# Another order of the branches and wider late products in a four-branch gated block

## The chip, the cores and the metric

One core of a Trainium2 chip. The metric is the device time of one execution in microseconds (us), the median of several runs. A profile is one execution taken by the hardware profiler; its span runs from the first to the last instruction. TensorE is written PE in the profile (PEld its weight loads), VectorE DVE, ScalarE ACT, GpSimd POOL, SyncE SP.

## What is computed

One layer over 256 tokens of width 2048. The input is RMS-normed and multiplied by a wide matrix `w_in`; the columns feed four recurrent branches of width 1024 (a: HGRN-2, b: S5, c: RWKV-7, d: Mamba-2), a z gate for each, and a sigmoid gate of width 2048 for each. Cut to what matters:

```python
h = rmsnorm(res, norm_pre[l])
(q_a, f_a, i_a, z_a, u_b, z_b, rkvwa_c, z_c, xbc_d, dt_d, z_d, gate_pre) = project_partitioned(h, w_in[l], IN_SPLITS)
o_a = hgrn2_branch(q_a, f_a, i_a, lb_all[l], hgrn_norm[l]) * silu(z_a)
o_b = s5_branch(u_b, ...) * silu(z_b)      # ends in g * sigmoid(g @ w_glu + b_glu)
o_c = rwkv7_branch(rkvwa_c, ...) * silu(z_c)
o_d = mamba2_branch(xbc_d, dt_d, z_d, ...)  # gated by silu(z_d) inside
for b in range(4):
    gate = sigmoid(gate_pre[..., b * 2048:(b + 1) * 2048] + gate_bias[l, b])
    merged += gate * (outs[b] @ w_up[l, b])
res = res + rmsnorm(merged @ w_out[l], norm_post[l])
```

All of it is float32 to near its full precision: each operand of a product is split into a high and a low part of the type float32r, and three products are summed (high x high, high x low, low x high).

## The kernel before

**The weight stream.** The weights are cut into units, each a block of output columns, and the units into 444 chunks of 512 KB. A chunk goes through four steps: SyncE issues its load into one of 3 buffers `raw` (`load`, line 1572); ScalarE copies the high part `hi` and VectorE subtracts to get `lo` (`split`, line 1584, into one of 4 buffers each); TensorE does the products into the PSUM tile `pg` of the unit (`products`, line 1595; two `pg` in turn, so a unit's PSUM must be free when the next but one begins). The loop (`loop`, line 1695) runs one step per chunk: the split of a chunk three ahead, the next load, the products, the evacuation of finished units, then branch work. A product always shows as line 261, an ACT instruction as line 207, a DVE tensor_tensor as line 216 and a scalar_tensor_tensor as line 229, since helpers issue them; the tile names tell them apart.

There are two kinds of units. A token-major unit (tm: gates, ups, z of a and d, HGRN's values, the output) has tokens as rows and 512 weight columns: a chunk is 12 matmuls of 512 columns; a unit from `w_in` or `w_out` has 8 chunks, an up unit 4. A feature-major unit (fm) has 256 features as rows and the 256 tokens as columns; the stationary operand is the weight. Its activations lie as one row of 512: 256 columns of high parts, then 256 of low ones. For each of its contraction tiles k and both f (128 features each) it does

```python
K.mm(ps[..., f, :], hi[:, kk, fs], m[:, 0:256], start=first, stop=False)
K.mm(ps[..., f, :], hi[:, kk, fs], m[:, 256:512], start=False, stop=False)
K.mm(ps[..., f, :], lo[:, kk, fs], m[:, 0:256], start=False, stop=last)
```

24 matmuls of 256 columns per chunk; 4 chunks (16 contraction tiles) per unit from `w_in`, 2 chunks (8 tiles) for the four `glu` units. The two f lie in two PSUM banks, of which they use the first half.

**The order of the units** is a list (chunks in brackets): u x4 of S5 (16), dt (2) and xbc x8 (32) of Mamba, wd (2), k x4, r x4 and v x4 of RWKV (48), q x4 and f x4 (32) and i x2 (16) of HGRN: 148 chunks. Then for d and after it for c: z (16), and four times gate and up (8 + 4 each). Then z of a (16), four gates of a (32), z of b (16), four ups of a, three gates of b, `glu` x4, the last gate of b, four ups of b, the output.

**Evacuation.** When a unit is done a generator takes it out of PSUM: `u_done` stores a copy and two parts to DRAM, `conv_done` does Mamba's convolution and stores, `shift_done` RWKV's token shift (k and r stay in SBUF, v is stored), `zfm_done` a SiLU from PSUM to `zs`, `glu_done` two sigmoids from PSUM to `ev`.

**Branches as jobs.** The recurrences are generators too, emitted between the chunks. Their matmuls go to PSUM tiles `pb`, in the same TensorE queue as the stream's. A planner books each instruction's estimated end on each engine (`t_pe`, `t_act`, `t_dve`; a transfer is booked as 2.0 us and 220 GB/s, line 181). After each chunk `run_jobs` (line 1562) emits stages of the job with the best priority, as long as

```python
while max(K.t_dve, K.t_act) <= K.t_pe + AHEAD:
```

with `AHEAD = 3.7`. Every engine works its queue in order, so what is emitted ahead of a split, or ahead of a product, stands in front of it. All loads of branches go through POOL's queue once the stream runs (`SOFT`), the weights through SP's.

Who starts when: S5's set-up (`s5_setup`, priority 5) after the constants, then S5's tiles 0 to 3 in turn, tiles 4 to 7 after job `c`; `c` (`rwkv_branch`, priority 1) when RWKV's k units are done, waiting inside for r and v; Mamba's step sizes `dt` when the dt unit is done, its halves `d0` after `dt` and `d1` after `d0` (priority 0), when the xbc units are done; HGRN's halves `a0` after `c`, `a1` after `a0` (priority 3); `b`, the reload of S5's early tiles, after `a1`. A unit may have a `need`: the first product of an up unit waits, in emission, for the branch output times its z; if the job is not done by then, `finish` (line 1550) emits all the rest of it ahead of the product.

The tiles by which a job is known in the profile: RWKV `wda`, `bc` (its keys over their norms), `L`, `GB`, `XT`, `W`, `Y`, `oc` (its output); Mamba `mx`, `mbc`, `dk` (loads), `xst`, `xD`; HGRN `hT`, `E`, `oa`; S5 `s5p` and `cx` in set-up, `us`, `bs`, `ta`, `tb`, `cu` in the tiles, `ghl` its split output.

Of the kernel before, what the change touches and what calls it, by code (L numbers as in the profile page):

```python
# [15 lines left out]
AF = mybir.ActivationFunctionType  # L16
# [47 lines left out]
AHEAD = 3.7  # L64
SLACK = 1.0

# the functions that each activation table serves
# [6 lines left out]
class _Kern:  # L74
    """Pools, constants and instruction helpers shared by the weight stream and the branches."""
# [36 lines left out]
    @staticmethod  # L112
    def live(tiles):
        """How many of the tiles are still referred to; the others are dropped from the list."""
        for i in range(len(tiles) - 1, -1, -1):
            if sys.getrefcount(tiles[i]) <= 2:
                del tiles[i]
        return len(tiles)
# [4 lines left out]
    def wait(self, n):  # L123
        """Until n more slots are free."""
        for _ in range(100):
            if self.room(n):
                return
            yield BLOCKED

    def wait_banks(self, n):  # L130
        """Until n more PSUM banks are free."""
# [5 lines left out]
    def fm(self, name, n=2):  # L137
        """A feature-major [128, 4 n, 256] array, in tiles of four feature tiles."""
        return [self.big([128, 4, 256], name=f"{name}{j}") for j in range(n)]
# [22 lines left out]
    def book(self, engine, cost, out, ins):  # L162
        """Book an instruction: it starts when the engine is free and its operands are there."""
# [45 lines left out]
    def _dve(self, out, ins, ns):  # L209
        """Book a vector instruction; one that reads the last one's output waits for it."""  # L210
# [52 lines left out]
    def tr(self, out, in_, b=0):  # L263
        """out = in_ transposed; in_ starts at partition b."""
# [12 lines left out]
    def ld(self, out, in_):  # L277
        """A transfer whose source may still be under way."""
# [3 lines left out]
    def ldx(self, out, in_):  # L282
        """A load of what has long been in DRAM."""
# [5 lines left out]
    def st(self, out, in_):  # L289
        """A store of what the scalar engine has just written."""  # L290
# [11 lines left out]
    def split(self, hi, lo, src):  # L302
        """src (float32 in SBUF) as the exact sum of two float32r parts."""
# [3 lines left out]
    def rstd(self, out, ss, n, eps):  # L307
        """out = 1 / sqrt(ss / n + eps), small tiles."""
# [5 lines left out]
def setup_consts(K):  # L314
# [24 lines left out]
    # ind[:, g, :] sums each half of the partitions into rows 2 g and 2 g + 1 of 32  # L339
# [15 lines left out]
    # lmask[s, level, t]: s and t (mod 64) are paired at that level of the binary split; level 0 is the diagonal  # L355
# [26 lines left out]
def head_sum(K, ps, i, sq):  # L382
    """Sums over each head's features of tile i, to rows 32 (i % 4) + 2 (i // 4) + half of ps."""
# [4 lines left out]
def bcast_heads(K, dst, src):  # L388
    """src DRAM [4, 4, 256] to dst (two tiles [128, 4, 256]): row (q, 2 g + e) on the 64 partitions of half e."""
# [5 lines left out]
# ---------------------------------------------------------------- RWKV-7  # L395
def rwkv_branch(K, rw):
    """rw: r, k, v (two tiles [128, 4, 256]) and wda [128, 256], after the token shift. Leaves K.o['c']."""
# [94 lines left out]
    # L1[c][e]: on the 64 key partitions of head parity e, rows (a | r) scaled by the decay;  # L492
    # on the other 64 partitions the masked products of k with them
# [37 lines left out]
    for c in range(4):  # L531
# [34 lines left out]
        # token-major copies of the scaled keys  # L566
# [89 lines left out]
    # Ws[e]: on the key partitions (state | U), on the other half (V | V)  # L656
# [31 lines left out]
    for q in range(2):  # L688
# [13 lines left out]
        for o in range(2):  # L702
# [11 lines left out]
            # the A^T blocks are no longer needed: their place takes the right-hand sides  # L714
# [88 lines left out]
# ---------------------------------------------------------------- HGRN-2  # L803
def hgrn_bounds(K):
    """The lower bounds of the forget gates, [128, 8 feature tiles]: log lb, -log lb, log(1 - lb), 1 - lb."""
    lg = K.parv("lb")
    t = K.sm([128, 5, 8], "lb")
    # softmax and running sum over the one layer, then minus the first layer's
# [19 lines left out]
def hgrn_half(K, g, load):  # L828
    """Heads 4g..4g+3: q, f [128, 4, 256] feature-major, v [128, 2, 512] token-major. Leaves K.o['a', g]."""
# [52 lines left out]
    # scores^T: the 64 x 64 diagonal blocks in accd, both off-diagonal kinds in acc and soff  # L882
# [111 lines left out]
def tail_tm(K, o, j, norm, ohl):  # L994
    """Block j (512 features) of a token-major output [128, 2, 512]: transpose, scale by norm, split."""
# [18 lines left out]
# ---------------------------------------------------------------- Mamba-2  # L1014
def mamba_steps(K, dtr):
    """Step sizes and decays of all heads from dt [16, 256]; token-major in K.mtm, running sums also in DRAM."""
# [15 lines left out]
    # dt = softplus(raw + bias) = max(x, 0) + log1p(exp(-|x|)), log1p(e) = 2 atanh(e / (2 + e))  # L1032
# [41 lines left out]
def mamba_half(K, g, load):  # L1074
    """Heads 8g..8g+7: x [128, 4, 256], bcx [128, 4, 256] (two groups' B, then C). Leaves K.o['d', g]."""
# [91 lines left out]
def mamba_tail(K, j, zs):  # L1167
    """Gate block j (512 features, two groups) and normalise; zs = silu(z) [128, 2, 512]."""
# [16 lines left out]
# ---------------------------------------------------------------- S5  # L1185
def exp_exact(K, out, x, t, ti):
    """out = exp(x) to float32 rounding: 2^k exp(r); t: two scratch tiles, ti: an int32 one."""
# [8 lines left out]
    # exp(r) = 1 + (r + r^2 / 2! + ... + r^9 / 9!)  # L1196
# [1092 lines left out]
```

## Time and profile before

| | |
|---|---|
| median of 3 runs | 1430.18 us (1429.64 to 1430.91) |
| profiled execution, span | 1427.8 us, 24645 instructions |
| profiled execution, what lies around the span | not listed; the median is 2.4 us above the span |
| PE / PEld / DVE / ACT / POOL busy | 97 / 86 / 73 / 58 / 11% of the span |
| bytes moved | 288.62 MB, mean 202 GB/s |
| matmuls of the stream with 512 columns | 393 ns mean for one (line 261, `pg<-hi,h`) |
| with 256 columns | 286 ns mean for one (`pg<-h,hi`) |

Matmuls are pipelined: the time of one overlaps the next, so the spacing of their starts is what a matmul takes from TensorE's time, not its duration. A wait is put down to the instruction that released it, in the form "engine tile line <- engine tile line: us in total, times, longest". In a table by stages a row is a stretch in us from the span's start, its length, the busy time and count of each engine, the granted TensorE clock, the DMA engines' busy share and GB/s. A row of a tile gives the count, min/median/max duration in ns, and the first and last start in us.

### The profile page before, as it was taken

Reading aid. Unit: us, or ns where it says so; the run is one execution under the profiler, and the core shown is the slowest. Engines: PE = TensorE matmul, PEld = TensorE weight load, DVE = VectorE, ACT = ScalarE, POOL = GpSimd, SP = SyncE. Lnnn points to the kernel's source line nnn. Section 1 sums busy time; section 2 is a strip of 40 time slices with the busy share of each in tenths; the row PEclk is TensorE's granted clock in tenths of the full one; section 3 lists DMA queues with packets and bytes.
Section 4 is the critical chain, followed back from the end, with each engine's and each line's share of the span. In section 5 each row is a group of like instructions: output and inputs, shape, how many; then the busy total and the mean of one; then the engine's idle time right before and its main releaser. Section 6 shows DMA issues by size and latency. Waiting matters only on the chain.

```text
span 1427.8 us, 24645 instructions
## 1 busy us (share of the span) xinstructions
PE 1390.9 (97%) x9751; PEld 1223.2 (86%) x9751; DVE 1038.0 (73%) x1422; ACT 827.1 (58%) x1136; POOL 162.0 (11%) x268
## 2 busy tenths in 40 slices
PE   8999989989999999999999999999999999999997
PEld 7999989989989887888789888888789987888886
DVE  6787488778786784576787699767978788576655
ACT  5455445845456546765578765787556444544442
POOL 6232310010025320011100001000010000000000
PEclk9999999999999999999999999999999999999999
DMA  7878985487657876477876567655686856676664
GB/s 214 239 240 263 279 270 163 135 191 232 206 155 175 228 236 179 142 203 201 232 207 198 181 207 197 211 177 172 193 197 194 214 177 191 213 267 194 183 195 135
DMA packets 199040, 288.62 MB, mean 202 GB/s; under 512 B 12453, under 2 KB 116750, under 8 KB 198926
## 3 DMA queue, kind: packets, MB, share of 16 engines
q1 hardware_dynamic: 169614, 237.15, 54.2%
q0 software_dynamic: 25216, 43.05, 13.9%
q10 hardware_dynamic: 4096, 6.86, 1.4%
q8 instruction: 76, 1.25, 0.3%
q14 instruction: 38, 0.31, 0.1%
HBM read 268.33 MB, written 18.66 MB: 201 GB/s over the span
## 4 chain that ended last, share of the span: by engine, by line
PE 71%; DMA 8%; DVE 8%; issue 6%; ACT 6%; POOL 0%; SPq 0%; ACTq 0%; DVEq 0%; POOLq 0%
PE pg L261 63%; PE pb L261 6%; DMA raw<-in_w_in_dram 6%; DVE lo L216 4%; ACT hi L207 2%; PE pb L267 1%; DVE ta L216 1%; ACT L207 1%; DMA cn<-in_s_c_im_dram 1%; DMA x<-in_x_dram 1%; DVE invtmp L216 0%; ACT hT L207 0%; DVE tb L243 0%; DVE tb L216 0%; DMA ds5b<-bl 0%
## 5 line engine op out<-in xcount | busy, mean ns | idle before, releaser
L216 DVE TENSOR_TENSOR lo<-raw,hi 128x1024 fp32r<-128x1024 f32 x444 | 541.1, 1223 | 350.6 <-ACT hi L207 342.3
L207 ACT ACTIVATE hi<-raw 128x1024 fp32r<-128x1024 f32 x444 | 465.9, 1055 | 532.7 <-PE pg L261 249.1
L261 PE MATMUL pg<-h,hi 128*128 128x256 f32 x2624 | 480.8, 286 | 4.1 <-DVE ev L229 3.6
L261 PE MATMUL pg<-hi,h 128*128 128x512 f32 x1408 | 448.1, 393 | 0.1
L261 PEld LDWEIGHTS pg<-h,hi 128*128 128x128 f32 x2624 | 409.9, 192 | 10.7 <-issue 6.9
L261 PE MATMUL pg<-h,lo 128*128 128x256 f32 x1312 | 371.6, 285 | 5.0 <-DVE lo L216 4.1
L261 PEld LDWEIGHTS pg<-hi,h 128*128 128x128 f32 x1408 | 264.9, 188 | 58.5 <-issue 2.5
L261 PE MATMUL pg<-lo,h 128*128 128x512 f32 x704 | 275.5, 391 | 2.6 <-DVE lo L216 2.4
L261 PEld LDWEIGHTS pg<-h,lo 128*128 128x128 f32 x1312 | 251.0, 192 | 6.7 <-DVE lo L216 5.4
L261 PE MATMUL pg<-hi,o 128*128 128x512 f32 x512 | 164.2, 394 | 0.0
L261 PEld LDWEIGHTS pg<-lo,h 128*128 128x128 f32 x704 | 132.6, 188 | 30.5 <-DVE lo L216 4.5
L261 PEld LDWEIGHTS pg<-hi,o 128*128 128x128 f32 x512 | 96.1, 188 | 21.9 <-issue 1.6
L261 PE MATMUL pg<-lo,o 128*128 128x512 f32 x256 | 99.8, 390 | 0.0
L261 PE MATMUL pg<-hi,mhl 128*128 128x512 f32 x224 | 71.1, 391 | 0.0
L280 POOL DMA_DIRECT2D gb<-in_gate_bias_dram x16 | 8.7, 545 | 541.1 <-DVE gate L216 477.9
L207 ACT ACT_TABLE_LOAD x51 | 65.4, 1283 | 5.3 <-DVE mss L235 2.8
L261 PEld LDWEIGHTS pg<-lo,o 128*128 128x128 f32 x256 | 48.1, 188 | 9.5
L261 PEld LDWEIGHTS pg<-hi,mhl 128*128 128x128 f32 x224 | 42.1, 188 | 8.7
L261 PE MATMUL pg<-lo,mhl 128*128 128x512 f32 x112 | 43.6, 389 | 0.0
L243 DVE TENSOR_TENSOR_SCAN tb<-s5p,ta 128x256 f32<-128x256 f32 x64 | 41.7, 701 | 0.1
L261 PEld LDWEIGHTS pg<-lo,mhl 128*128 128x128 f32 x112 | 21.0, 188 | 4.2
L261 PE MATMUL pg<-ghl,hi 128*128 128x256 f32 x128 | 23.1, 283 | 0.0
(371 smaller groups left out, 1362.6 us busy)
## 6 DMA issues: line engine op xcount, KB each, us to landing
raw<-in_w_in_dram SPq DMA_DIRECT2D x340, 512.0 KB
raw<-in_w_up_dram SPq DMA_DIRECT2D x64, 512.0 KB
raw<-in_w_out_dram SPq DMA_DIRECT2D x32, 512.0 KB
us<-duhl POOLq DMA_DIRECT2D x16, 256.0 KB, 6.4
bs<-ds5b POOLq DMA_DIRECT2D x16, 256.0 KB, 7.6
gb<-in_gate_bias_dram POOLq DMA_DIRECT2D x16, 256.0 KB, 4.7
raw<-in_s_w_glu_dram SPq DMA_DIRECT2D x8, 512.0 KB
x<-in_x_dram SPq DMA_DIRECT2D x4, 512.0 KB
```

The source lines that it names most:

```text
L207: return self.nc.scalar.activation(out=out, in_=in_, func=func, **kw)
L216: return self.nc.vector.tensor_tensor(out=out, in0=in0, in1=in1, op=op)
L243: return self.nc.vector.tensor_tensor_scan(out=out, data0=data0, data1=data1, initial=0.0, op0=ALU.mult, op1=ALU.add)
L261: return self.nc.tensor.matmul(out, lhsT, rhs, start=start, stop=stop, **kw)
L267: return self.nc.tensor.transpose(out, in_, self.ident[b:b + p, b:b + p])
L280: return self.nc.gpsimd.dma_start(out=out, in_=in_)
```

## The change

Five things; comments and docstrings also go.

- The order of the first units: one u unit, then RWKV's wd, k, r, v, then the other three u units, dt and xbc, then HGRN's as before. The sum is the same 148 chunks; k is done after 22 chunks, r after 38, v after 54.
- The order of the jobs: `d0` starts after `c` (before: after `dt`), `a0` after `d1` (before: after `c`). `d1` follows `d0` and `a1` follows `a0` as before.
- The order of the late units: branch c ahead of branch d, and by written strings of z, gates (g) and ups (u) in place of z and four times gate, up. The first up product of c is chunk 188, that of d chunk 244.
- `AHEAD` goes from 3.7 to 3.0.
- The eight z units of b and c and the four glu units become wide: the high weights multiply all 512 columns in one matmul, into a whole PSUM bank, the low weights the first 256; in the evacuation `join` copies the second half out (ACT) and adds the first (DVE), and the SiLU or the sigmoids read the sum from SBUF.

```diff
-AHEAD = 3.7
+AHEAD = 3.0
...
-                u.ps = u.ps[:, 0:u.nc_ // 128, 0:256]
+                u.ps = u.ps[:, 0:u.nc_ // 128, 0:512 if u.wide else 256]
...
+                    pf = ps[0:u.cols or 128, f, :]
+                    if not u.wide:
+                        K.mm(pf, hi[:, kk, fs], m[:, 0:256], start=first, stop=False)
+                        K.mm(pf, hi[:, kk, fs], m[:, 256:512], start=False, stop=False)
+                        K.mm(pf, lo[:, kk, fs], m[:, 0:256], start=False, stop=last)
+                        continue
+                    if not last:
+                        K.mm(pf, hi[:, kk, fs], m, start=first, stop=False, skip_group_check=True)
+                    K.mm(pf[:, 0:256], lo[:, kk, fs], m[:, 0:256], start=False, stop=False, skip_group_check=True)
+                    if last:
+                        K.mm(pf, hi[:, kk, fs], m, start=False, stop=True, skip_group_check=True)
...
+    def join(ps, name="ev"):
+        if ps.shape[2] == 256:
+            return ps
+        t = K.big([128, ps.shape[1], 256], name=name)
+        K.act(t, ps[:, :, 256:512], AF.Copy)
+        K.add(t, ps[:, :, 0:256], t)
+        return t
...
-            zs = K.big([128, 2, 256], name="zs")
+            zs = join(ps, "zs") if ps.shape[2] == 512 else K.big([128, 2, 256], name="zs")
             yield 0
-            K.act(zs, ps, AF.Silu)
+            K.act(zs, zs if ps.shape[2] == 512 else ps, AF.Silu)
...
-            ev = K.big([128, 2, 256], name="ev")
+            wide = ps.shape[2] == 512
+            ev = join(ps) if wide else K.big([128, 2, 256], name="ev")
+            if wide:
+                yield 0
             for f in range(2):
-                K.act(ev[:, f, :], ps[:, f, :], AF.Sigmoid, bias=K.par("b_glu", 2 * j + f))
+                K.act(ev[:, f, :], (ev if wide else ps)[:, f, :], AF.Sigmoid, bias=K.par("b_glu", 2 * j + f))
...
-    for j in range(4):
-        add(_Unit("fm", w_in, KT, C_UB + 256 * j, 256, hmv, u_done(2 * j)))
...
-        S.start("d0", mamba_half(K, 0, load_mamba), 0, 0, after="dt")
+        S.start("d0", mamba_half(K, 0, load_mamba), 0, 0, after="c")
...
+    for j in range(1):
+        add(_Unit("fm", w_in, KT, C_UB + 256 * j, 256, hmv, u_done(2 * j)))
...
+    for j in range(1, 4):
+        add(_Unit("fm", w_in, KT, C_UB + 256 * j, 256, hmv, u_done(2 * j)))
+    add(_Unit("fm", w_in, KT, C_DT, 128, hmv, dt_done))
...
-        S.start("a0", hgrn_half(K, 0, load_hgrn), PRIO_A, 0, after="c")
+        S.start("a0", hgrn_half(K, 0, load_hgrn), PRIO_A, 0, after="d1")
...
-    for b, key in ((3, "d"), (2, "c")):
-        z_units(b, key)
-        for j in range(4):
-            gate_unit(b, j)
-            up_unit(b, j, b == 3, False)
+    for b, key, order in ((2, "c", ORDER_C), (3, "d", ORDER_D)):
+        g = iter(range(4))
+        u = iter(range(4))
+        for what in order:
+            if what == "z":
+                z_units(b, key)
+            elif what == "g":
+                gate_unit(b, next(g))
+            else:
+                up_unit(b, next(u), b == 2, False)
...
+    for u in U:
+        u.wide = u.kind == "fm" and u.nc_ == 256 and u.done.__name__ == "done" and u.done.__qualname__.split(".")[-3] in WIDE
...
+WIDE = ("zfm_done", "glu_done")
+ORDER_C = "ggzguguuu"
+ORDER_D = "zgguguguu"
```

More of the change, by code (lines that the diff above doesn't have):

```diff
@@ L1498, in __init__ @@
         self.cols = None
+        self.wide = False
         self.held = []
@@ L1643, in products @@
                     fs = slice(128 * f, 128 * f + (u.cols or 128))
-                    K.mm(ps[0:u.cols or 128, f, :], hi[:, kk, fs], m[:, 0:256], start=first, stop=False)
-                    K.mm(ps[0:u.cols or 128, f, :], hi[:, kk, fs], m[:, 256:512], start=False, stop=False)
-                    K.mm(ps[0:u.cols or 128, f, :], lo[:, kk, fs], m[:, 0:256], start=False, stop=last)
+                    pf = ps[0:u.cols or 128, f, :]
[9 more added lines that the diff above has]
+                        K.mm(pf, hi[:, kk, fs], m, start=False, stop=True, skip_group_check=True)
         self.ends[j] = K.t_pe
@@ L1829, in done @@
             S.finish("consts")
+            ps = join(ps)
+            yield 0
             tmp = K.big([128, 2, 256], name="ev") if dst in spilled else None
@@ L1863, in done @@
         def done(ps):
+            ps = join(ps)
+            yield 0
             t = K.big([128, 2, 256], name="ev")
@@ L1874, in done @@
                           ALU.mult, ALU.add)
+            del ps
             yield 1
@@ L1883, in done @@
         def done(ps):
+            if ps.shape[2] == 512:
+                K.ld(spilled[key][:, i0:i0 + 2], join(ps))
+                return
             ev = K.big([128, 2, 256], name="ev")
@@ L2025, in done @@
         def done(ps):
-            ev = K.big([128, 2, 256], name="ev")
+            wide = ps.shape[2] == 512
+            ev = join(ps) if wide else K.big([128, 2, 256], name="ev")
+            if wide:
+                yield 0
             for f in range(2):
-                K.act(ev[:, f, :], ps[:, f, :], AF.Sigmoid, bias=K.par("b_glu", 2 * j + f))
+                K.act(ev[:, f, :], (ev if wide else ps)[:, f, :], AF.Sigmoid, bias=K.par("b_glu", 2 * j + f))
             def post():
@@ L2120, in dt_done @@
         S.start("dt", mamba_steps(K, dtr), 0)
-    add(_Unit("fm", w_in, KT, C_DT, 128, hmv, dt_done))
-    U[-1].cols = 16
-    for j in range(8):
-        add(_Unit("fm", w_in, KT, C_XBC + 256 * j, 256, hmv,
-                  conv_done("x" if j < 4 else "bc", 2 * (j % 4), 2 * j, start_mamba if j == 7 else None)))
+    for j in range(1):
+        add(_Unit("fm", w_in, KT, C_UB + 256 * j, 256, hmv, u_done(2 * j)))
     add(_Unit("fm", w_in, KT, C_WD, 128, hmv,
@@ L2136, in hybrid_block_kernel @@
                                  then if j == 3 else None)))
+    for j in range(1, 4):
+        add(_Unit("fm", w_in, KT, C_UB + 256 * j, 256, hmv, u_done(2 * j)))
+    add(_Unit("fm", w_in, KT, C_DT, 128, hmv, dt_done))
+    U[-1].cols = 16
+    for j in range(8):
+        add(_Unit("fm", w_in, KT, C_XBC + 256 * j, 256, hmv,
+                  conv_done("x" if j < 4 else "bc", 2 * (j % 4), 2 * j, start_mamba if j == 7 else None)))
     for key, c in (("q", C_QA), ("f", C_FA)):
```

## The prediction

> **What bounds the kernel now.** I read the page's first two parts, then the waits of TensorE, the table by stages, the chain of waits at the waits, and the transfers around them.
>
> ```profile
> span 1427.8 us, 24645 instructions
> ...
> PE 1390.9 (97%) x9751; PEld 1223.2 (86%) x9751; DVE 1038.0 (73%) x1422; ACT 827.1 (58%) x1136; POOL 162.0 (11%) x268
> ```
>
> ```profile
> PE pg L261 <- DVE lo L216: 6.5, 8, 2.2
> PE pb L267 <- DMA npt<-in_norm_pre_dram: 4.0, 1, 4.0
> PE pg L261 <- DVE ev L229: 3.6, 1, 3.6
> PE pb L261 <- DVE cu L216: 2.7, 1, 2.7
> PE pb L261 <- DVE tb L216: 2.6, 2, 2.4
> PE pb L261 <- DVE diag L234: 2.5, 1, 2.5
> PE pb L267 <- DVE cx L235: 2.1, 1, 2.1
> ...
> PE pg L261 <- DVE evm L1833: 0.8, 1, 0.8
> ```
>
> TensorE's queue is the bound: it is busy 97% of the span, and VectorE, next, 73%. The second block (who waited: total us, times, longest) holds nearly all its waiting. The rows shown add to 24.8 us; npt and diag (6.5) are the start, before any weight product, so 18.3 us is what another order of the work can reach. These waits cost more than they last:
>
> ```profile
> 157.30:160.60 3.30, 3.24 (x16) 3.27 (x17) 2.40 (x2) 2.46 (x4) 0.00 (x0) 0.50 0.54 157
> 184.60:187.90 3.30, 3.30 (x18) 3.30 (x17) 1.67 (x2) 2.90 (x6) 0.00 (x0) 0.50 1.03 360
> 314.40:317.60 3.20, 3.15 (x14) 3.15 (x15) 3.20 (x3) 0.88 (x2) 0.00 (x0) 0.50 1.01 323
> 420.20:423.40 3.20, 3.20 (x18) 2.38 (x13) 2.53 (x4) 0.00 (x0) 0.00 (x0) 0.50 0.86 269
> 543.00:546.30 3.30, 3.30 (x55) 2.75 (x48) 2.22 (x2) 1.05 (x1) 1.04 (x2) 0.50 0.81 243
> ```
>
> In this table by stages (stretch, PE, PEld, DVE, ACT, POOL, granted clock, DMA share, GB/s) the clock is at 0.50 in five stretches of over 3.2 us, each behind one of the longer waits (cx, ev, lo, tb, cu). Half speed for 3.3 us loses 1.65 us, five times 8.3 us. So some 18.3 + 8.3 = 27 us lie in the order of the work; the rest is products, which only fewer or better spaced matmuls shorten.
>
> **The change part by part.**
>
> *Wide products.* Eight z units and four glu units put the 512 columns of (high | low) through one matmul and the low weights through a second, instead of three matmuls of 256. The timeline of TensorE has the spacing of both kinds:
>
> ```profile
> 1082.93 0.28 PE L261 MATMUL pg<-h,lo 128*128 128x256 f32 x1
> ...
> 1083.29 0.28 PE L261 MATMUL pg<-h,lo 128*128 128x256 f32 x1
> ```
>
> ```profile
> 1200.29 0.39 PE L261 MATMUL pg<-lo,h 128*128 128x512 f32 x1
> ...
> 1200.97 0.39 PE L261 MATMUL pg<-lo,h 128*128 128x512 f32 x1
> ```
>
> Between two equal matmuls lie three: 0.36 us for three of 256 columns, 120 ns each; 0.68 us for three of 512, 227 ns each. A pair (contraction tile, 128 features) costs 360 ns now and 227 + 120 = 347 ns then: 13 ns less. The z units have 16 x 2 pairs, the glu units 8 x 2: 8 x 32 + 4 x 16 = 320 pairs, **-4.2 us**, all on the path. The Trainium skill (TensorE: Matmul & The Clock Gate, Back-to-back issue gap) gives N / 2.4 + 2.5 ns for an isolated matmul: 109 and 216 ns, so 327 against 325 ns per pair and an estimate of 0.8 us in all; the trace's 120 and 227 disagree with it by 11 ns each, and the measurement decides.
>
> The halves are then joined: an ACT copy and a DVE add per unit, nearest rows:
>
> ```profile
> L207 ACT ACTIVATE ev<-pg 128x512 f32<-128x512 f32 x12 | 7.1, 589 | 0.1
> L216 DVE TENSOR_TENSOR yo<-pg,np 128x512 f32<-128x512 f32 x7 | 4.8, 686 | 2.3 <-ACT junk L207 2.3
> ```
>
> ```profile
> 1079.00:1127.00 48.00, 48.00 (x407) 47.19 (x406) 40.02 (x50) 25.28 (x33) 4.33 (x7) 1.00 0.86 214
> 1240.00:1263.00 23.00, 23.00 (x193) 22.96 (x192) 15.64 (x17) 13.92 (x18) 2.65 (x5) 1.00 0.67 201
> ```
>
> 12 x (0.59 + 0.69) = 15.4 us of work. In the stretches of the z units of S5 (four units in 48 us) and of glu (four in 23 us) DVE idles 8.0 and 7.4 us, and the adds take 4 x 0.69 = 2.7 us. A unit's PSUM is wanted again a whole unit later (5.5 us for glu, 11 for z), so I cost the join at nothing; uncovered it would be up to 15.4 us.
>
> *Mamba-2 behind RWKV-7.* The `ev` wait is where Mamba's loads start:
>
> ```profile
> 168.57 10.76 DMA raw<-in_w_in_dram
> ```
>
> ```profile
> mx<-dx POOLq DMA_DIRECT2D x2, 512.0 KB, 8.7
> dk<-dacs POOLq DMA_DIRECT2D x2, 512.0 KB, 8.0
> mbc<-dbc POOLq DMA_DIRECT2D x3, 256.0 KB, 8.4
> ```
>
> The first row is the chain of waits, the others the transfers issued from 160 to 185 us (size, median us to landing). Mamba's 2.8 MB and S5's first tile share the engines with the weights; one weight chunk takes 10.76 us, the splits follow late, and the evacuation (`ev`) that PSUM waits for comes later still. With `d0` waiting for `c` these loads leave this place: -3.6 - 1.65 = **-5.3 us**. Kept end: 0, if another transfer does the same.
>
> *S5's units 1 to 3 behind RWKV's.* Their stores (a copy and two parts) leave the start:
>
> ```profile
> 28.40:66.10 37.70, 35.64 (x289) 1.00 0.81 232
> ```
>
> ```profile
> duhl<-uhl POOLq DMA_DIRECT2D x12, 128.0 KB, 5.6
> du<-ev ACTq DMA_DIRECT2D x3, 256.0 KB
> ```
>
> 289 weight products are 12 chunks of 24: 37.7 us for 12 x 2.88 = 34.6, so 3.1 us are lost. RWKV's k and r stay in SBUF and store nothing. I take half, **-1.5 us** (0 to -3.1). The same stores then meet S5's tile loads some 150 us later; at the same price 0 to +3.1, taken as 0, since Mamba's 2.8 MB no longer stand there.
>
> *VectorE's lead 3.7 to 3.0.* Branch work is issued only while the planned VectorE and ScalarE are less than this ahead of TensorE, so at most 0.7 us less stands in front of a split. Eight waits on `lo`: 0 to 8 x 0.7 = 5.6 us; the longest hang on transfers, so I take **-2**. The price is later branch work, which must still end before the product that needs it:
>
> ```profile
> L207 ACT ACTIVATE wda<-wda x1: 400/400/400, 256.8 to 256.8; 64x256 f32<-64x256 f32 x1
> L216 DVE TENSOR_TENSOR L<-r,sw x16: 406/416/423, 334.5 to 374.7; 64x256 f32<-64x256 f32 x16
> L216 DVE TENSOR_TENSOR oc<-oc,bb x2: 1217/1221/1225, 735.0 to 738.4; 128x1024 f32<-128x1024 f32 x2
> L216 DVE TENSOR_TENSOR xD<-xD,xst x2: 691/691/691, 235.3 to 300.1; 128x512 f32<-128x512 f32 x2
> L216 DVE TENSOR_TENSOR oa<-oa,zs x2: 1216/1217/1218, 959.1 to 1066.2; 128x1024 f32<-128x1024 f32 x2
> L261 PE MATMUL pg<-hi,o x512: 387/389/504, 598.9 to 1330.6; 128*128 128x512 f32 x171
> ```
>
> Rows give first and last start. RWKV runs from 256.8 to 739.6 us: 78 us to its scaled rows (`L`), 405 from there. Now it starts when k is done, after 22 chunks (4 of u, 2, 16), some 14 + 22 x 3.2 = 85 us, so it ends near 85 + 78 + 405 = 568. Its first up product is chunk 188 of the new stream; in the old one the first up product is chunk 172 at 598.9, and 16 more chunks at 2.72 are 642. That leaves 74 us. Mamba (loads at 169.8, end 300.8: 131 us) then ends near 699; its first up product is 56 chunks later, 642 + 152 = 794. HGRN took from RWKV's end to 1067.4, 328 us, and ends near 1027, 40 us earlier than now; its place in the stream is unchanged. So I cost the smaller lead at nothing.
>
> *RWKV's bursts, now early.* RWKV's normalised keys (eight scalar_tensor_tensor, 3.25 us) stood right in front of a split:
>
> ```profile
> 310.01 3.25 DVE L229 SCALAR_TENSOR_TENSOR bc<-k,pt,bc 128x256 f32<-128x256 f32 x8
> 313.18 1.22 DVE L216 TENSOR_TENSOR lo<-raw,hi 128x1024 fp32r<-128x1024 f32 x1
> ```
>
> ```profile
> 122.50:174.20 51.70, 49.64 (x402) 49.45 (x402) 30.00 (x44) 26.80 (x36) 8.74 (x13) 0.97 1.00 262
> 300.00:352.00 52.00, 49.07 (x400) 47.81 (x399) 41.68 (x69) 22.16 (x36) 3.27 (x6) 0.97 0.92 237
> ```
>
> Here it cost `lo`'s 2.2 us, `evm`'s 0.8 and the clock's 1.65: 4.7. It moves to about 140 us, where S5's set-up holds the transfers at a share of 1.00 against 0.92, and its loads come on top. Between 0 (no wait: -4.7) and twice more (+9.4) I take **+2**.
>
> The order of gates, z and ups in the tail moves equal work among equal chunks: 0. The waits cu, tb and cx belong to jobs that stay: 0.
>
> Sum: -4.2 - 5.3 - 1.5 - 2 + 2 = -11.0; span 1416.8. The median of the runs, 1430.18, is 2.4 above the profiled span: **1419**.
>
> **The rivals.**
> 1. *The waits only change places.* Five waits and five half-clock stretches under any order, since the planner's transfer times stay as optimistic (2.0 us and 220 GB/s: 4.4 us for 512 KB, against the 8.7 above); only the matmuls count: 1430.2 - 4.2 = 1426. For it: the waits come from five different jobs, of which the change removes one. Against: Mamba's and RWKV's transfers no longer come close together.
> 2. *The waits nearly vanish.* If the longer chain and smaller lead clear the 27 us but for 4: 1430.2 - 4.2 - 23 = 1403. For it: after 732 us TensorE hardly waits. Against: the start stays crowded.
> 3. *Slower: RWKV's start and S5's set-up share 85 to 180 us.* That stretch has a DMA share of 1.00 already, and RWKV brings lora weights and the two broadcasts. If each of its four bursts there (keys, bonus rows, scaled rows, Gram) costs what the keys cost at 310 us plus a late weight chunk's 3.6, 8.3 each, 33 us come and 4.7 go; with -4.2, -5.3 and -2 this is 1430.2 + 33 - 16.2 = 1447. It decides from two such bursts on (16.6 against 16.2).
> 4. *The skill's spacing holds*, the wide units give 0.8: 1422.5. The 120 and 227 ns speak against it.
> 5. *Nothing moves*: the join or the new collisions eat the 4.2: 1430.
>
> **How the numbers follow.** Forecast 0.45 (own range 1412 to 1424), rival 1 0.19, rival 2 0.13, rival 3 0.13, rival 4 0.02, rival 5 0.08. Changes under 0.2%, 2.9 us, can't be told from none here. Rival 1 is 4.2 below, so three quarters of it count as faster. Faster: 0.45 + 0.14 + 0.13 + 0.02 = 0.74; same 0.05 + 0.08 = 0.13; slower 0.13. The range reaches from rival 2's 1403 to 1437, half way into rival 3.
>
> **What would show it.** Spacing: pairs of 347 ns in z and glu, joins between. No wait on `ev` with a half-clock stretch near 180 us. RWKV's `oc` near 570 us, Mamba's last `xD` near 700, HGRN's last `oa` near 1030. Wrong if TensorE's waits on `lo` between 85 and 200 us exceed the 6.5 us of now, if RWKV ends after 642 us (its rest would then be forced ahead of the up product), or if the table by stages shows more than five half-clock stretches.

## The result, and the profile after

The changed kernel takes 1442.58 us (median of 5 runs, 1440.12 to 1446.74) against 1430.18 before on the same chip (1422.95 to 1433.26): a ratio of 1.0096, interval 1.0074 to 1.0118. (The ratio is the record's estimate from all runs, 13.7 us; the two medians alone lie 12.4 us apart.) It is slower, where 11 us less were forecast. The profiled execution is the longest of the five, 1446.74 us, with a span 17.2 us longer than before's, so its account overstates the typical loss by some 4 us.

The page of the changed kernel:

```profile
span 1445.0 us, 24050 instructions
...
PE 1400.2 (97%) x9431; PEld 1215.5 (84%) x9431; DVE 1047.0 (72%) x1434; ACT 828.4 (57%) x1144; POOL 159.6 (11%) x268
```

320 matmuls are gone, 12 ACT copies and 12 DVE adds have come (ACT counts only 8 more, since it has four table loads fewer). TensorE is the bound as before. The timeline of TensorE in a z unit of branch c shows the new spacing (start, us, engine, line, tiles):

```profile
605.86 0.39 PE L261 MATMUL pg<-h,hi 128*128 128x512 f32 x1
606.09 0.28 PE L261 MATMUL pg<-h,lo 128*128 128x256 f32 x1
...
607.24 0.39 PE L261 MATMUL pg<-h,hi 128*128 128x512 f32 x1
```

Four pairs lie between the first and the last row: 1.38 us, 345 ns a pair (347 forecast, 360 before). The 4.2 us were gained. They were lost again in TensorE's waits (who waited: total us, times, longest):

```profile
PE pg L261 <- ACT hi L207: 8.0, 3, 3.9
PE pb L267 <- DVE cx L235: 4.7, 1, 4.7
...
PE pg L261 <- DVE o L216: 3.4, 2, 2.3
PE pb L261 <- issue: 3.2, 2, 2.5
PE pb L261 <- ACT bkT L207: 3.2, 2, 2.9
PE pg L261 <- DVE lo L216: 3.0, 4, 0.8
...
PE pb L267 <- ACT GB L207: 1.7, 1, 1.7
```

All rows of this view add to 36.3 us, before to 28.2. The waits on `ev`, `tb` and `cu` have gone or shrunk and those on `lo` have halved; `hi`, `o`, `bkT` and `GB` are new and `cx` has grown. The half-clock stretches, by the table by stages:

```profile
11.70:15.10 3.40, 3.40 (x16) 3.40 (x17) 2.88 (x7) 1.90 (x5) 3.05 (x9) 0.50 0.56 161
138.00:144.80 6.80, 6.34 (x28) 6.04 (x29) 5.35 (x11) 2.78 (x4) 2.97 (x5) 0.50 1.01 343
250.60:254.00 3.40, 3.40 (x18) 3.40 (x17) 2.67 (x5) 1.31 (x2) 0.00 (x0) 0.51 0.48 139
431.60:441.80 10.20, 10.20 (x133) 10.14 (x130) 3.48 (x4) 7.60 (x13) 0.00 (x0) 0.50 0.68 205
585.20:592.00 6.80, 6.25 (x20) 5.38 (x21) 5.30 (x7) 4.96 (x6) 0.00 (x0) 0.50 0.64 198
615.90:619.30 3.40, 3.40 (x12) 2.84 (x11) 2.04 (x3) 1.29 (x2) 0.00 (x0) 0.50 0.75 206
670.50:673.90 3.40, 3.40 (x9) 2.61 (x9) 3.40 (x5) 0.46 (x2) 0.00 (x0) 0.50 0.67 220
```

37.4 us at half speed lose up to 18.7 (an estimate: half of the time); before it was five stretches and 8.3. So -4.2 + 8.1 (waits) + 10.4 (clock) = 14.3 of the 17.2 us. The other 2.9 are about the amount (3.0 us in sum) by which the starts of the branches' own matmuls lie further apart, with waits and half clock taken out; no single row explains it.

The chain of waits says what five of the waits hung on:

```profile
125.83 6.88 DMA bc<-dinv
132.99 5.05 DMA ds5b<-bl
...
239.69 9.37 DMA cn<-in_s_c_im_dram
...
567.06 19.76 DMA raw<-in_w_in_dram
...
598.12 10.04 DMA raw<-in_w_in_dram
```

Every one is a transfer that came late while a branch's burst stood beside it; that the burst made it late is read from the place, not shown by a run. At 125 us RWKV's four broadcasts `bc` (256 KB each) meet S5's set-up stores, and a weight chunk comes late (`hi` wait of 3.25 us, then 6.8 us at half clock). At 240 us a load of S5's set-up lands after 9.37 us, behind the four `duhl` stores of a moved u unit and two stores of its own. At 567 us a weight chunk takes 19.76 us from issue to use, behind two chunks that are still under way in its own queue and beside RWKV's and S5's loads, and TensorE waits 3.94 us. At 598 us Mamba's loads delay a chunk by 10.04 us, in their new place. The largest branch transfers issued from 560 to 590 us:

```profile
bb<-dbon POOLq DMA_DIRECT2D x4, 256.0 KB, 13.5
v<-drv POOLq DMA_DIRECT2D x2, 512.0 KB, 11.2
us<-duhl POOLq DMA_DIRECT2D x2, 256.0 KB, 8.6
bs<-ds5b POOLq DMA_DIRECT2D x2, 256.0 KB, 9.8
```

They bring 3 MB beside the weights. The jobs end later than forecast too (first and last start of a tile):

```profile
L216 DVE TENSOR_TENSOR L<-r,sw x16: 406/415/423, 164.3 to 203.9; 64x256 f32<-64x256 f32 x16
L216 DVE TENSOR_TENSOR oc<-oc,bb x2: 1218/1220/1221, 648.9 to 653.7; 128x1024 f32<-128x1024 f32 x2
L216 DVE TENSOR_TENSOR xD<-xD,xst x2: 691/692/692, 707.2 to 756.9; 128x512 f32<-128x512 f32 x2
L216 DVE TENSOR_TENSOR oa<-oa,zs x2: 1218/1218/1219, 975.6 to 1101.0; 128x1024 f32<-128x1024 f32 x2
L216 DVE TENSOR_TENSOR ghl<-cu,ghl x4: 417/418/421, 919.2 to 1261.3; 128x256 fp32r<-128x256 f32 x4
```

RWKV's scaled rows (`L`) begin at 164, as forecast (85 + 78 = 163). Its output ends at 655 instead of 568, the first up product of c stands at 663, and there TensorE waits 3.4 us on `o`, that output times its z, which is emitted ahead of the product.

### The profile page after: what moved, and what is told of

It is laid out like the page before. It is cut to its first block, busy times and chain, and to the rows that moved or that the text cites. A ratio compares the mean times of both kernels' runs of the same rounds, so it can differ in the third digit from the quotient of the medians.

```text
span 1445.0 us, 24050 instructions
## 1 busy us (share of the span) xinstructions
PE 1400.2 (97%) x9431; PEld 1215.5 (84%) x9431; DVE 1047.0 (72%) x1434; ACT 828.4 (57%) x1144; POOL 159.6 (11%) x268
## 4 chain that ended last, share of the span: by engine, by line
PE 77%; DMA 7%; DVE 6%; ACT 6%; issue 4%; POOL 0%; ACTq 0%; SPq 0%; DVEq 0%
PE pg L261 68%; PE pb L261 7%; DMA raw<-in_w_in_dram 3%; DVE lo L216 3%; ACT hi L207 3%; DMA raw<-in_w_up_dram 2%; PE pb L267 1%; ACT L207 1%; DMA cn<-in_s_c_im_dram 1%; DMA x<-in_x_dram 1%; DMA bc<-dinv 0%; DVE ta L216 0%; ACT hT L207 0%; DVE tb L243 0%; ACT zs L207 0%
## 5 line engine op out<-in xcount | busy, mean ns | idle before, releaser
L261 PE MATMUL pg<-h,hi 128*128 128x256 f32 (+2 forms) x2368 | 483.2, 300 | 8.0 <-ACT hi L207 8.0
L261 PEld LDWEIGHTS pg<-h,hi 128*128 128x128 f32 (+1 forms) x2368 | 380.7, 193 | 24.4 <-ACT hi L207 9.1
L261 PEld LDWEIGHTS pg<-hi,o 128*128 128x128 f32 x512 | 96.7, 189 | 24.5 <-DVE o L216 4.2
L280 POOL DMA_DIRECT2D us<-duhl x16 | 10.3, 645 | 128.2 <-PE pb L261 49.4
```

Source lines behind the costliest of these rows:

```text
L261: return self.nc.tensor.matmul(out, lhsT, rhs, start=start, stop=stop, **kw)
L280: return self.nc.gpsimd.dma_start(out=out, in_=in_)
```

## The experiments

The ratios are to the kernel before on the same chip. The last two columns are from the profiled execution: the total of TensorE's waits, and the time at a granted clock of 0.50 without the stretch at the very end (up to half of it is lost). These two carry chance: the six kernels of the new order with lead 3.0 and three buffers issue the same instructions up to some 600 us, and yet their profiles show 20.6 to 24.5 us of waits and 17.1 to 23.9 us at 0.50 ahead of the 164th split, which starts at 570.5 to 574.3 us. In the old order the six kernels with lead 3.7 and three buffers reach that split at 547.4 to 555.8 us.

| kernel | ratio (95% interval) | waits | at 0.50 |
|---|---|---|---|
| before | 1 | 28.2 | 17.1 |
| changed | 1.0096 (1.0074 to 1.0118) | 36.3 | 37.5 |
| after_narrow: new order, no wide units | 1.0056 (1.0037 to 1.0075) | 29.0 | 20.5 |
| after_zc_narrow: new order, c's z narrow | 1.0053 (1.0032 to 1.0073) | 29.4 | 23.9 |
| after_narrow_ahead37: new order, lead 3.7 | 1.0124 (1.0104 to 1.0145) | 37.0 | 30.7 |
| after_ahead37: changed, lead 3.7 | 1.0154 (1.0132 to 1.0176) | 43.4 | 34.1 |
| after_up_later: ups of c later | 1.0242 (1.0222 to 1.0262) | 50.6 | 44.4 |
| before_ahead30: old order, lead 3.0 | 1.0180 (1.0158 to 1.0202) | 43.2 | 34.1 |
| before_wide: old order, 12 wide | 1.0065 (1.0042 to 1.0089) | 33.5 | 27.3 |
| before_zc_narrow: old order, 8 wide | 0.9992 (0.9978 to 1.0007) | 27.5 | 20.5 |
| before_wide_s54 | 1.0132 (1.0112 to 1.0152) | 40.1 | 27.3 |
| before_wide_glu_later | 1.0126 (1.0103 to 1.0149) | 48.1 | 44.4 |
| before_raw4: fourth raw buffer | 0.9985 (0.9966 to 1.0004) | 27.3 | 30.7 |
| after_raw4 | 1.0026 (1.0008 to 1.0044) | 32.2 | 27.3 |
| before_wide_unbooked | 1.0062 (1.0041 to 1.0083) | 33.3 | 20.5 |
| after_unbooked | 1.0051 (1.0032 to 1.0070) | 36.3 | 30.7 |
| before_wide_raw4 | 0.9979 (0.9964 to 0.9994) | 26.5 | 23.9 |
| after_wide_raw4 | 1.0037 (1.0019 to 1.0056) | 32.0 | 13.7 |
| after_late_silu | 1.0079 (1.0060 to 1.0098) | 36.0 | 30.7 |
| before_wide_raw4_late | 0.9974 (0.9959 to 0.9989) | 23.2 | 23.9 |

**The parts alone.** The theories: the order gained nothing, or the joins cost, or the lead did.

before_wide: the kernel before with the wide units and joins only. 

> The kernel before with the wide products and their joins alone (its order, its lead of 3.7). Theory A (the new order of branches costs the time; wide products pay what the spacing says): 320 pairs x 13 ns = 4.2 us faster than before, ratio 0.997. Theory B (the smaller lead costs the time): the same 0.997. Theory C (the joins cost more than the spacing saves): ratio 1.000 to 1.005, with waits of TensorE on splits in the z units of c and b and in glu.

The old order loses by them, 1.0065, more than theory C had (up to 1.005), and not on splits in the z units and `glu`, where it put the waits. TensorE's waits and the stretch around them:

```profile
PE pb L261 <- DVE ta L216: 5.7, 2, 5.3
...
PE pb L261 <- DVE tb L216: 4.9, 3, 2.4
```

```profile
1236.40:1246.60 10.20, 6.54 (x27) 3.92 (x28) 5.97 (x8) 3.17 (x4) 0.54 (x1) 0.50 0.40 129
```

```profile
L216 DVE TENSOR_TENSOR ghl<-cu,ghl x4: 416/421/425, 987.0 to 1245.0; 128x256 fp32r<-128x256 f32 x4
```

`ta` and `tb` belong to S5's last tile, whose rest is emitted right ahead of the first `glu` product, at 1243.0. In the kernel before that product stood at 1240, and `ghl` ended at 1222:

```profile
L216 DVE TENSOR_TENSOR ghl<-cu,ghl x4: 415/418/419, 928.8 to 1222.3; 128x256 fp32r<-128x256 f32 x4
```

S5 ends 23 us later. The joins are booked on ScalarE and VectorE, so less branch work should be emitted per chunk; the runs below test that.

before_ahead30: `AHEAD = 3.0` in the kernel before. 

> The kernel before with the lead 3.0 in place of 3.7, nothing else. Theory A: within 0.3% of before, RWKV's output oc within 10 us of its 739.6. Theory B: slower by 8 to 12 us (1.006 to 1.008), oc some 30 us later or more waits ahead of it.

```profile
PE pb L261 <- DVE ta L216: 13.2, 3, 9.0
```

The same tile misses the same product by more (`ghl` ends at 1264). The smaller lead alone costs the old order 1.8%, over twice what theory B had (0.6 to 0.8%), and `oc` is 17 us later instead of 30.

after_ahead37: `AHEAD = 3.7` in the changed kernel. 

> The changed kernel with the lead back at 3.7. Theory A: stays near 1.010 (1.006 to 1.013), the waits on weight chunks behind RWKV's and Mamba's loads and the long half-clock stretch near 430 us still there. Theory B: back to 0.997 to 1.000, RWKV's oc done by 620 us in place of 656, no wait on its z products.

after_narrow: `WIDE = ()` in the changed kernel. 

> The changed kernel with narrow products in all units (no joins). Theory A and B: 4.2 us slower than the changed kernel, ratio 1.0125 to before. Theory C: as fast as the changed kernel or faster, ratio 1.010 or less.

after_narrow_ahead37: both. 

> The new order alone: narrow products and the lead of 3.7. If the order itself costs time whatever the lead: 1.005 to 1.012, with waits behind transfers between 110 and 260 us. If the order pays and the lead and the wide products spoil it: 0.995 to 1.000.

In the new order the smaller lead helps, by 0.6 to 0.7% with and without joins: after_ahead37 is slower than either theory had it, and theory B, by which the larger lead would win the loss back, fails. after_narrow is as theory C had it: the joins cost more than the spacing saves. The order with its lead, without joins, is 0.56% slower than before: about 8 us that the forecast had as 6.8 us of gain. The two can't be priced one without the other: at a lead of 3.7 the order costs 1.24% (1.0124 against 1), at 3.0 it wins 1.2% (1.0056 against 1.0180). The waits of after_narrow add to 29.0, against 28.2: in sum they only change places. The chunk that is late at 567 us is late here too:

```profile
565.16 21.57 DMA raw<-in_w_in_dram
```

after_zc_narrow: four of the changed kernel's wide units, c's z, made narrow. 

> The changed kernel with narrow products in the four z units of c, wide ones in the z units of b and in glu (192 pairs, 2.5 us). Theory N: the joins in c's z units put RWKV's end off (654 against 636 us); without them oc ends near 636, no wait on o, ratio 1.003 to 1.006. Rival (the wide products or joins are slow wherever they are): 1.008 to 1.009, two fifths of the way back to the narrow kernel's 1.0056.

```profile
L216 DVE TENSOR_TENSOR oc<-oc,bb x2: 1219/1220/1220, 631.1 to 635.9; 128x1024 f32<-128x1024 f32 x2
```

RWKV ends 18 us sooner, no wait on `o` is left, and the ratio falls to that of after_narrow. As far as the intervals tell, the whole loss by the joins comes from these four units. They stand just ahead of the product that needs RWKV. The place of the loss bears it out: from the start of the 164th split to that of the 212th, the gates, z and ups of c (48 chunks, counted by `hi<-raw`), the changed kernel takes 163.3 us, this one 152.1 and after_narrow 152.0.

before_zc_narrow: the same in the old order. 

> The kernel before with wide products in the z units of b and in glu alone (192 pairs). Theory N (a job that ends after the product that needs it is forced in front of it): nothing is changed ahead of the z units of b, S5's last ghl ends by 1232, some us ahead of glu's first product, so no wait there, and the 2.5 us of the spacing show: ratio 0.996 to 1.000. Rival (wide products or joins are slow in themselves): 1.003 to 1.005.

No wait on `ta` or `tb` near `glu` is left, and the loss of before_wide is gone. So in the old order too the four z units of c make it, between 720 and 785 us, though the wait stands at 1232. The 8 wide units would give 2.5 us by their spacing; the measured 0.9992 can't be told from 1.

**Moving the need or the job.** If the miss is the cause, a later need or an earlier job should bring the 4.2 us.

after_up_later: `ORDER_C = "ggzgguuuu"`. 

> The changed kernel with branch c's late units as gate gate z gate gate up up up up: its first up product stands 8 chunks (22 us) later. Theory N (jobs end after the product that needs them, so their rest is forced in front of it): the waits of TensorE on o (3.4 us at 663 to 670) and the half-clock stretch behind them go, 5 to 7 us faster than the changed kernel, ratio 1.005 to 1.006. Theory T (transfers of branches that delay weight chunks are all of it): unchanged, 1.009 to 1.010.

before_wide_s54: S5's tile 4 started at priority 2 instead of 5. 

> The kernel before with the wide products, and S5's tile 4 ahead of HGRN in priority (2 in place of 5), so that S5's chain should end some 10 to 30 us earlier; HGRN, with 30 to 59 us to spare, later by a tile's 15. Theory N: the wait of 8.2 us and the 10.2 us at half clock at 1232 to 1246 go, and the 4.2 us of the wide products show: ratio 0.995 to 0.999. Rival (the wide products or joins are slow in themselves): 1.004 to 1.007 as without it.

before_wide_glu_later: `gb3` ahead of `glu` and the last up of a behind it, with the operands of a kept for it. 

> The kernel before with all 12 wide units, and in the stream the last gate of b ahead of glu and the last up of a behind it: glu comes 4 chunks (10.9 us) later, with 4 chunks in place of 8 between it and the ups that need it. Theory N: against the wide kernel of the old order S5's tile 7 is done in time, the 8.2 us of waits and 5 us of half clock at 1232 to 1246 go: ratio 0.996 to 1.000, or up to 4 us more if the ups of b now wait for z. Rival: 1.005 to 1.008 as before.

All three lost by more than either of their theories had, and in the first two another job misses its product:

```profile
PE pb L261 <- DVE ta L216: 11.8, 2, 11.0
```

```profile
PE pb L267 <- DVE oa L216: 6.3, 1, 6.3
```

The first row is of after_up_later: no wait on `o`, but S5's tile misses `glu`. The second is of before_wide_s54: S5 is in time, HGRN's output misses the first up of a. In before_wide_glu_later the kept operands took four slots that S5's tiles wait for, so `ta` became 16.0 us; it tells nothing of a later need. (That the slots are the reason is read from the code.) VectorE and ScalarE have one sum of time for jobs: what one job is given early, the next one lacked in these runs.

**Slack.** A fourth buffer for raw chunks lets weights be loaded earlier, and one branch slot pays for it.

```diff
-NSLOT = 37
+NSLOT = 36
-RAW_BUFS = 3
+RAW_BUFS = 4
```

after_raw4: on after_zc_narrow. 

> The changed kernel with narrow products in c's z units, and four buffers for raw weight chunks in place of three (36 slots for branches in place of 37): a weight load is issued one chunk, 2.9 us, earlier. Theory T (in the new order the rest of the loss, 1.0053, is weight chunks that come late behind bursts of branch loads at 125, 567 and 598 us): each of these waits shorter by up to 2.9 us, 5 to 10 us faster, 0.998 to 1.002. Rival (the bursts are as long as before and only the place differs; waits stem from the branches' own results): 1.003 to 1.008.

before_raw4: on the kernel before. 

> The kernel before with four raw buffers and 36 slots. Theory T: its waits on late chunks at 180 and 308 to 312 us (ev 3.6, lo 2.2, and two half-clock stretches) shrink, 4 to 8 us faster, 0.994 to 0.997. Rival: 0.999 to 1.004.

before_wide_raw4: on before_wide. 

> The kernel before with the twelve wide units and a fourth buffer for raw weight chunks (one branch slot less). With four buffers alone S5 ended at 1202 us, 40 us ahead of glu, against 1222 with three. Slack theory (the wide products pay where the jobs end early enough for the joins): no forced job, ghl near 1220 us, ratio 0.994 to 0.998, below both 1 and the four buffers alone (0.9985). Rival (the joins' own work costs): ratio 1.002 to 1.006.

after_wide_raw4: on the changed kernel. 

> The changed kernel with a fourth buffer for raw weight chunks (one branch slot less). With narrow c units and four buffers (1.0026) RWKV ended at 627 us, HGRN at 1031 and S5 at 1205. Slack theory: RWKV ends by 642 us, no wait on o, ratio 1.000 to 1.003. Rival (the joins' own work): ratio over 1.005.

In the old order S5 ends 20 us earlier with four buffers (`ghl` 1202), and in the new one, with c's z narrow, RWKV ends at 628 and HGRN at 1032. The ratios of after_raw4 and before_raw4 fall between their two theories and speak for neither. In the old order the wide units then cost nothing that can be seen: 0.9979 with all twelve against 0.9985 without. In the new one RWKV ends at 632 and no wait on `o` is left, as the slack theory had it, but 1.0037 is above its range. The expectation for before_wide_raw4 named the ratio rightly and the milestone wrongly:

```profile
L216 DVE TENSOR_TENSOR ghl<-cu,ghl x4: 418/419/426, 978.1 to 1243.0; 128x256 fp32r<-128x256 f32 x4
```

S5's last part starts after the first `glu` product (1237.1), but just ahead of the contraction tiles that need it, and TensorE has no long wait. The new order is still 0.58% behind the old one with the same buffers (1.0037 against 0.9979), so most of its loss is not that of the joins. (The profiled execution of after_wide_raw4, 1429.57 us, is among its shortest; its median is 1434.62.)

**What of the join costs.** Two ways: its work, or its booking. The unbooked kernels run the joins and set the planner's times back afterwards.

```diff
+        kept = K.t_act, K.t_dve, K.last, K.stage_end
...
         K.act(t, ps[:, :, 256:512], AF.Copy)
         K.add(t, ps[:, :, 0:256], t)
+        K.t_act, K.t_dve, K.last, K.stage_end = kept
+        K.done_at[t.tensor.name] = K.done_at[ps.tensor.name]
...
```

before_wide_unbooked: 

> The kernel before with the twelve wide units, whose joins run but are not booked: after the copy and the add the planner's times of ScalarE and VectorE are set back, so the jobs should be emitted as without joins. Booking theory (the joins cost by delaying the jobs' emission, so that S5's last tile is forced ahead of the first glu product): no wait on ta or tb near 1232 to 1240 us, ghl ends near 1225 us, ratio 0.996 to 1.000. Rival (the joins' own 15.4 us of ScalarE and VectorE work costs): S5 still ends near 1240 us or splits come late, ratio 1.004 to 1.007 as with booking (1.0065).

after_unbooked: 

> The changed kernel with its joins run but not booked. Booking theory: RWKV ends near 636 us as with narrow units (654 with booked joins), no TensorE wait on o at 663 to 668 us, HGRN's oa ends near 1072 us, ratio 1.002 to 1.005. Rival (the joins' own work): oc near 650 us, waits on o stay, ratio near 1.009 as in the changed kernel.

The booking theory had its milestones right in the old order: S5 is in time again (`ghl` 1229.5, product at 1247.2). In the new one they come half way: RWKV ends at 645, between its 636 and the 655 of the changed kernel, and HGRN at 1081 instead of 1072, but no wait on `o` is left:

```profile
L216 DVE TENSOR_TENSOR oc<-oc,bb x2: 1218/1218/1219, 639.0 to 643.6; 128x1024 f32<-128x1024 f32 x2
```

The new order wins back 0.45%, and the stretch of c takes 155.6 us instead of 163.3. The old one wins nothing back: 1.0062 is the ratio of the rival, though the milestones are those of the booking theory. One place where the join's work delays TensorE stands in the timeline of ScalarE in before_wide_unbooked (idle time in brackets):

```profile
782.09 0.58 ACT L207 ACTIVATE zs<-pg 128x512 f32<-128x512 f32 x1
785.87 0.63 ACT L207 ACTIVATE zs<-zs 128x512 f32<-128x512 f32 x1 [3.19 <-DVE zs L216]
786.41 3.29 ACT L207 ACTIVATE hT<-hT,lb 128x256 f32<-128x256 f32 x8
...
791.98 1.04 ACT L207 ACTIVATE hi<-raw 128x1024 fp32r<-128x1024 f32 x1
```

ScalarE copies, stands 3.19 us until VectorE has done the add (which stands in VectorE's queue behind four branch instructions and a `lo`), and does the SiLU. Nine branch instructions and a table load follow, and only then the split. TensorE waits 3.0 us for that split, and its clock is at 0.50 for 6.8 us from 792.5 on. So a join that isn't booked can delay a split; that this makes the whole 0.62% is not shown. In the changed kernel ScalarE idles on the add like this:

```profile
ACT zs L207 <- DVE zs L216: 10.0, 7, 2.2
ACT ev L207 <- DVE ev L216: 7.5, 4, 2.4
```

after_late_silu: the changed kernel with the SiLU and the sigmoids of a wide unit emitted a chunk after the join (`yield 1` in place of `yield 0`). 

> The changed kernel with the SiLU or sigmoids of a wide unit emitted a chunk after its join, so that ScalarE does not stand waiting for VectorE's add. In the changed kernel ScalarE idles 10.0 us (zs, 7 times) and 7.5 us (ev, 4 times) on that add. Theory of the round trip (copy on ScalarE, add on VectorE, SiLU on ScalarE, and the splits queued behind it): these two waits fall under 4 us together, the wait on o at 663 to 668 us shrinks, ratio 1.003 to 1.007. Booking theory (what the planner books for the join delays the jobs, whatever ScalarE waits for): ratio stays 1.008 to 1.011.

before_wide_raw4_late: the same on before_wide_raw4. 

> The kernel before with the twelve wide units, a fourth buffer for raw chunks, and the SiLU or sigmoids a chunk after the join. With four buffers and the wide units the ratio was 0.9979, ScalarE waiting 10.8 + 6.8 us on the add. Theory of the round trip: 0.995 to 0.9975. If the round trip is covered by the fourth buffer: 0.997 to 0.999, no difference.

The round trip shrinks as meant (`zs` 10.0 to 2.3 us; the wait on the sigmoids' add vanishes), and the wait on `o` is gone (`oc` ends at 641). The stretch of c takes 154.7 us, though the joins are booked as before. The ratio 1.0079 lies between the two theories, and its interval overlaps that of the changed kernel: little of the time won there is kept. HGRN's `oa` now delays TensorE 3.2 us at 977 and 1089 us, and from the 276th split to the last this kernel takes 497.4 us against 491.5. In the old order with four buffers S5 ends at 1203 with booked joins, as without any (1202):

```profile
L216 DVE TENSOR_TENSOR ghl<-cu,ghl x4: 418/419/419, 959.2 to 1203.0; 128x256 fp32r<-128x256 f32 x4
```

So what delays the jobs is not the booked work of the join alone: a SiLU that must wait for the add in the same chunk, in ScalarE's queue and in the planner's times alike, delays them too. Which of these two counts is not shown. In time 0.9974 can't be told from 0.9979. It is the fastest kernel of the study, and faster than before. Which share of its 0.26% the wide products have is not settled, since the four buffers alone have 0.15% with an interval that reaches 1.

## Why the prediction was wrong

Of the 24.7 us between forecast (-11.0) and result (+13.7), after_narrow divides off two parts. Order and lead, forecast at -5.3 - 1.5 - 2 + 2 = -6.8, brought +8.0: 14.8 us. The wide products with their joins, forecast at -4.2, brought +5.7: 9.9 us.

- **The products' spacing: right.** -4.2 forecast, 345 ns a pair measured.
- **The waits that the new order and lead clear (-5.3 - 1.5 - 2 + 2): the step that failed by most.** The forecast had waits and half clock fall by 6.8 us, with no others in their place. In after_narrow the waits went from 28.2 to 29.0 us and the time at half clock from 17.1 to 20.5: +0.8 and +1.7, so +2.5 us. By another 2.8 us in sum the starts of the branches' own matmuls lie further apart; no cause of that is known.
- **"So I cost the join at nothing": the second step that failed.** VectorE's idle share in the stretch was the wrong measure. A join delays the jobs, and the last job of a branch has a product that waits for it. RWKV's end went from 637 to 655 us (after_zc_narrow against changed) and the product stood at 663. Between 1.0053 and 1.0096 lie 6.1 us, and with the 1.7 us that the spacing of c's z wins (4 x 32 pairs by 13 ns) the four joins cost 7.8 us instead of 0. In the old order 1.0065 is 9.3 us, so the twelve cost 13.5. The bound "uncovered up to 15.4 us" holds both by luck: it is the joins' own work, and the loss came by the jobs that they delay.
- **"That leaves 74 us": the job times were carried over.** 405 us from `L` to RWKV's end came from a place where Mamba and S5's set-up were over. In the new place it took 491, and 473 with c's z narrow. The start, 163, was right; Mamba ended at 758 instead of 699 and HGRN at 1102 instead of 1027. So "I cost the smaller lead at nothing" had no ground either. The smaller lead wins 0.6 to 0.7% in the new order and loses 1.8% in the old one. Without wide units RWKV and HGRN end earlier by it in the new order (637 and 1073 against 649 and 1141), S5 later in the old one (1264 against 1222); why the sign turns stays open.
- **-5.3 for Mamba behind RWKV: its "kept end, 0" came true.** The `ev` wait is gone, but the same loads meet a weight chunk at 598 us; three waits of 0.8 us each and 3.4 us at half clock follow, 4.0 of the 5.3.
- **-1.5 for S5's units behind RWKV's: right at the start, paid back after it.** From 28.4 to 66.1 us there are now 312 weight products at full clock where 289 were: 23 x 0.12 = 2.8 us, near the upper end. The same stores, taken as 0 where they come later, precede the 9.37 us load of S5's set-up at 240 us, with 4.7 us of wait and 1.7 by the clock. But before, the same load took 8.52 us at 148 us, with 2.1 and 1.7: the net price is 2.6 us.
- **-2 for `lo`: right in size by luck.** 6.5 became 3.0 us, the longest 2.2 became 0.8, but the waits on `hi` took their place. With the lead alone changed the waits on splits (`lo` and `hi`) rise each time it falls to 3.0: from 6.5 to 10.4 us in the old order, from 6.8 to 11.8 in the new one without wide units, from 8.1 to 11.0 with them. The late chunk itself had not been priced.
- **+2 for RWKV's early bursts: right in size, not in its way.** At 134 us 3.25 + 0.46 + 3.4 by the clock come, and 4.7 go at 310. But the wait is on a weight chunk beside the broadcasts; the eight instructions of the keys, which were priced, now run at 142.67 us ahead of a split with no wait of TensorE behind them.
- **The rivals.** Rival 3's time (1447) is the nearest, its place is not. From 85 to 200 us TensorE is busier than before, and it is less busy in all three stages from 200 to 800 us. Stages before, then after:

```profile
85.00:200.00 115.00, 108.52 (x878) 107.67 (x877) 81.27 (x128) 61.70 (x84) 28.46 (x45) 0.97 0.94 274
200.00:400.00 200.00, 195.75 (x1719) 190.40 (x1718) 160.59 (x273) 109.31 (x161) 9.55 (x16) 0.99 0.66 186
400.00:600.00 200.00, 194.11 (x1590) 165.69 (x1590) 133.12 (x182) 123.49 (x188) 48.15 (x52) 0.98 0.69 189
600.00:800.00 200.00, 197.43 (x1416) 167.72 (x1416) 142.73 (x167) 137.89 (x183) 15.94 (x26) 1.00 0.72 202
```

```profile
85.00:200.00 115.00, 110.53 (x892) 106.41 (x892) 84.82 (x137) 63.90 (x105) 19.49 (x33) 0.97 0.69 208
200.00:400.00 200.00, 189.37 (x1631) 184.21 (x1630) 154.74 (x256) 114.33 (x162) 50.88 (x61) 0.99 0.76 207
400.00:600.00 200.00, 192.76 (x1833) 166.52 (x1832) 123.46 (x145) 112.63 (x169) 28.49 (x45) 0.96 0.81 195
600.00:800.00 200.00, 193.50 (x1046) 158.03 (x1046) 156.26 (x213) 118.20 (x156) 11.51 (x18) 0.98 0.68 203
```

Rival 1, the waits only change places, is what the new order without joins does in its waits (29.0 against 28.2). Yet its time was 0.56% longer, not the same. Of the three signs named as "wrong if", two came (RWKV after 642 us, more than five half-clock stretches); the first, `lo` between 85 and 200 us, did not.

Open stays why RWKV takes 491 us in its new place: that it shares VectorE with Mamba's convolutions and S5's set-up is argued, not shown. So does most of the 0.56% that the new order loses with its lead: the runs show its size, and that the waits only move, not what makes the rest.

## What to carry to other kernels

An engine with idle time is not free if a planner, or a chain of jobs with due times, spends that time: before an instruction is costed at nothing, find the job that ends nearest to its need and ask by how much it moves. A job's duration at one place in the stream (405 us here) need not hold at another (473 and 491). And a copy on one engine, an add on another and the next step on the first is a round trip in two ordered queues: everything behind it waits with it. Letting a chunk pass in between took most of ScalarE's wait away here, and brought the late jobs forward, without a gain in time that can be told from none; doing all of it on one engine was not run.

## What the runs showed of the hardware

- A short wait can cost far more than it lasts. Behind 2.50 us at 428 us the clock stood at 0.50 for 10.2 us, some 5 of them with matmuls of 32x32 (128 of them took 5.7 us from first to last start, against 3.7 at full clock before); behind 1.08 and 2.29 us at 664 and 668 it did so for 3.4. The Trainium skill (TensorE: Matmul & The Clock Gate, HAM oscillation — how this bites in real kernels) asks for no idle gap over about 3.4 us; these gaps are shorter, and the half clock came all the same.
- A weight chunk of 512 KB took 19.76 us from issue to use (21.57 in after_narrow) behind two chunks of its own queue and beside 3 MB of branch loads on another. Forecast bursts had been priced with 10.76 at most.
